# Order of the output products in two recurrent mixers

## The chip, the cores and the metric

The kernel runs on one core of a Trainium2 chip. The metric is the device time of one execution in microseconds. Of the kernel before there are three runs: 1267.03, 1274.09 and 1274.21 us, median 1274.09 us. Engines: PE is TensorE (PEld its weight loads), DVE VectorE, ACT ScalarE, POOL GpSimd, SP SyncE, which issues the DMAs.

## What is computed

One layer of a diffusion backbone in fp32, for 512 latent tokens of one request and 128 context tokens of another (640 in all, `NT`). A norm modulated by the conditioning, one input projection, four token mixers in parallel (pooling, Fourier, RWKV-7, GLA), a projection of each with a gated sum, an output projection, a second norm and an MLP. Cut to the two mixers that matter here:

```python
def step(S, inp):                                    # RWKV-7, a state of 64 x 64 for each of 4 heads
    sa = einsum('bhvk,bhk->bhv', S, -kk_t)
    S = S * w_t + sa[..., None] * (kk_t * a_t) + v_t[..., None] * k_t
    return S, einsum('bhvk,bhk->bhv', S, r_t)

def step(S, inp):                                    # GLA, a chunk at a time
    o = einsum('bhts,bhse->bhte', att, vc) + einsum('bhtd,bhde->bhte', qc * exp(bcum), S)
    S = exp(b_last)[..., None] * S + einsum('bhsd,bhse->bhde', kc * exp(b_last - bcum), vc)
    return S, o
```

Both run once forward and once backward over the tokens, and the two outputs are added. In both, an output is a sum of two products: one over the state that the chunk found (the "state product"), one over the tokens inside the chunk (the "token product").

## The kernel before

*The main stream.* All large matrix products are taken as three passes on a high and a low part of each operand. `load` fetches a block of weights by DMA (L241), `split` makes its two parts on ScalarE (L246) and VectorE (L247), and `terms` issues the passes (L368). The gates and the branch projections (`gate`, `branch`, `merged`) are such products too, and stand between the steps of the recurrent mixers in TensorE's instruction stream.

*The order.* Each engine works through its own list of instructions in order. A framework writes the lists when the kernel is built: it takes instructions by priority (the order of the program, with `hi()` ahead) and by its own estimate of when operands are ready. So the lists don't depend on the run, and an engine that reaches an instruction too early waits there with all that stands behind it.

*RWKV-7* (from L627) works on two heads at a time (`hp`), one in each half of the 128 partitions (`HR`, `par` 0 and 1), in chunks of 64 tokens. Everything that doesn't need the state is prepared for all chunks: `SL` and `AB` (products within a chunk, L772 to L778, from `big`, L756 to L758), the inverse `TT` and `BHT`. Then eight steps run over the chunks. The tile `x` holds for every chain and head the state over v's tokens and u's tokens over v's. A step does, on TensorE, `pp` (L910, state against `SL`), copied by VectorE (L913); `pu` (L924, against `TT`), copied by VectorE and ScalarE into `x` (L927, L928); and `pn` (L933, against `BHT`), added by VectorE to the decayed state (L939), which gives the `x` of the next step. GpSimd fills in the tokens of v (L847). Steps 0 and 1 work on four chains (forward and backward, of the latent and of the context tokens), steps 2 to 7 on two.

The outputs of a step are issued one step late (`late`), behind L933 and ahead of the next L910, those of the last two steps at the end. `outputs` writes one PSUM bank `po`: chain `i` has 64 columns, head `par` the partitions `HR[par]`. The state product (L898) has all 128 partitions as its rows and 64 columns, the token product (L899) the 64 partitions of its head and 64 columns. ScalarE copies the bank out (L901). With four chains these are 16 products, with two 8. After the last step the sum of both directions is normalised (L957 to L969).

*GLA* (from L974) prepares the products within tiles of 128 tokens (`att`, L1073 to L1080) and the states at the borders of the tiles (`st`, L1121 to L1126; L1129 for the final state), then sums the outputs (L1135 to L1148) for each half `j` of the channels into one PSUM bank for the four latent tiles and another for the context tile: two token products (L1142, one a head, 64 columns each) and, for the latent tiles, two state products over both directions (L1146). VectorE adds the bank to `og` (L1148); ScalarE squares it (L1159) for a norm whose sums are products again (L499).

Of the kernel before, what the change touches and what calls it, by code (L numbers as in the profile page):

```python
# [19 lines left out]
P = 128  # L20
D = 1024
KT = 8
NS = 512
# [4 lines left out]
EPS = 1e-6  # L28
# [32 lines left out]
def blocks(w, starts, n):  # L61
    """Blocks of n columns of w, each with a partition's rows next to one another."""
    return np.stack([w[:, c : c + n].reshape(-1, P, n).transpose(1, 0, 2) for c in starts])


def laid_out(x):
    """The weights and the small vectors in the order in which they are loaded."""
    return {
        "t_par": np.concatenate([np.reshape(x[n], (-1, P)) for n, _ in PARAMS]).T,
        "t_in": blocks(x["w_in"][0], W_TILES, P),  # L70
        "t_ada": blocks(x["ada_w"][0], range(0, 6 * D, 512), 512),
        "t_branch": np.stack([blocks(w, range(0, D, P), P) for w in x["w_branch"][0]]),
        "t_w1": blocks(x["mlp_w1"][0], range(0, FF, P), P),
        "t_w2": np.stack([blocks(x["mlp_w2"][0][r : r + 256], (0, 512), 512) for r in range(0, FF, 256)]),
        "t_out": blocks(x["w_out"][0], (0, 512), 512),
    }
# [60 lines left out]
def backbone(ctx, tc, a, y_prompt, y_sample, out_rwkv, out_gla):  # L137
# [6 lines left out]
    turn = [0]  # L144

    def first():
        """Ahead of all else, in the order of the calls."""
        turn[0] += 1
        return tc.high_priority(offset=1000000 - 1000 * turn[0])
# [7 lines left out]

# [1 line left out]
    cst = cpool.tile([P, NCST], F32, name="cst")  # L159
# [37 lines left out]

# [1 line left out]
    sc = cpool.tile([P, 2, KT], F32, name="sc")  # L199
# [29 lines left out]
    def blocks(src, pool=None, tag="w", bufs=2):  # L229
        """A block of weights, 128 rows to each k, as tiles for its two parts and a list of loads."""  # L230
        pool = wpool if pool is None else pool
        _, n, c = src.shape
        wh = pool.tile([P, n, c], F32R, name=tag + "h", tag=tag + "h", bufs=bufs)
        wl = pool.tile([P, n, c], F32R, name=tag + "l", tag=tag + "l", bufs=bufs)
        m = min(n, 512 // c)
        return wh, wl, [(src[:, k : k + m], wh[:, k : k + m], wl[:, k : k + m]) for k in range(0, n, m)]
# [7 lines left out]
    def split(raw, wh, wl):  # L244
        """Two parts that the tensor engine takes in one pass each."""
        S.copy(wh, raw)  # L246
        V.tensor_tensor(wl, raw, f32(wh), ALU.subtract)  # L247
# [15 lines left out]
    def ada_out(pc, part, hf, out):  # L263
        """(2, 512) sums, as columns [P, 4, 2], plus the bias and, for a scale, one, times the norm's gain."""
        kts = slice(hf * 4, hf * 4 + 4)

        def wide(t, o):
            return t[:, o + hf * 4 : o + hf * 4 + 4].unsqueeze(2).broadcast_to([P, 4, 2])

        if part in (1, 4):  # L270
            V.tensor_tensor(out[:, kts], pc, wide(bp1, part * 8), ALU.add)
            V.tensor_tensor(out[:, kts], out[:, kts], wide(pcol, PC["norm1_g" if part == 1 else "norm2_g"]), ALU.mult)
        else:
            V.tensor_tensor(out[:, kts], pc, wide(pcol, PC["ada_b"] + part * 8), ALU.add)

    def ada_mm(pool, pt, hf, part, k):
        """Two steps of half of the scale (1) or of the shift (0): rows of c and c_ctx, by the parts of sc."""
        raw = raws[part, hf, k]
# [12 lines left out]
    def ada_cols(pool, pt, hf):  # L291
        """The rows of the scale and the shift as per-partition columns."""
        with hi():
# [17 lines left out]
    def ada_sum(pt, acc, part, hf, out):  # L311
        """The sums over the partitions, as columns."""
        for k in range(4):
# [5 lines left out]
    def ada_rest(pool, bank, part, hf, bufs=2):  # L319
        """Half of another part, summed per partition on VectorE; returns what sums over the partitions."""  # L320
        c0 = part * D + hf * 512
# [19 lines left out]

# [1 line left out]
    def rstd_of(pool, ss, n):  # L343
        """1/sqrt(ss / D + EPS): a guess of its negative from the exponent's bits, and Newton steps that turn the sign."""
        h, y, z = (pool.tile([P, n], F32, name=f"rs{j}", tag=f"rs{j}", bufs=2) for j in range(3))
# [17 lines left out]
    def terms(pt, wh, wl, k, c0, mh, ml, start, stop):  # L363
        """pt += W.T @ m for one tile of 128 rows of W; wh/wl tiles [P, K, cols]."""
        lh, ll = wh[:, k, c0 : c0 + P], wl[:, k, c0 : c0 + P]
# [107 lines left out]

# [1 line left out]
    def proj(c0):  # L475
# [18 lines left out]
    def bank_pair(lhsT, rhs, bank=None):  # L494
        """Two banks of lhsT.T @ rhs over the two halves of the tokens."""
        r = []
# [9 lines left out]
    def rsqrt_of(lhs, eps, sqs, rss, bank=None):  # L506
        """rs = 1/sqrt(lhs.T @ sq + eps)."""
        for sq, rs in zip(sqs, rss):
# [5 lines left out]

# [1 line left out]
    apool = pf_.enter_context(tc.tile_pool(name="apool", bufs=1))  # L516
# [39 lines left out]

# [1 line left out]
    # Over the sample's tokens, the sums and the differences of t and NS - t: cosines of the ones, sines of the others.  # L558
    zc = [ft(512).rearrange("p (s j c) -> p s j c", s=2, j=2) for _ in range(3)]
# [38 lines left out]

# [1 line left out]
    uscr = [dpool.tile([P, NT], F32, name=f"uscr{n}") for n in range(len(UC))]  # L600
# [25 lines left out]

# [1 line left out]
    psa.close()  # L628
# [53 lines left out]
    def pick(t, step, smp):  # L682
        """The two directions' chunks of one step, of the samples or of the prompt."""
        return t[:, step : step + 13 : 12] if smp else t[:, 8 + step : 11 + step : 2]

    for hp in range(2):
# [65 lines left out]
        def pair(d, e, g0, g1):  # L752
            """(k, b, k) of a group of chunks, scaled by e."""
            n = g1 - g0
# [33 lines left out]

        # the 32x32 diagonal blocks of I - A, inverted with one block per partition
        ivf = upool.tile([80, 1024], F32, name="inv", tag="inv")  # L790
# [30 lines left out]

        # tokens of v per chunk
        vr = ut()
# [17 lines left out]
        def new_x(step):  # L841
            """Per chain and head: the state over v's tokens, and u's tokens over v's."""
            x = upool.tile([P, 4, 2, 2, 64], F32, name="xc", tag="xc", bufs=3)
# [45 lines left out]

        # the recurrence over the chunks  # L890
        O = [ut(), ut()]

        def outputs(x, live):
            po = pxc()
            for i, d, c in live:
                for par, R in enumerate(HR):
                    o64 = slice(i * 64, i * 64 + 64)
                    PE.matmul(po[R, o64], lhsT=x[:, i, par, 0, :], rhs=SL[d][:, par, c, 64:128], start=True, stop=False)  # L898
                    PE.matmul(po[R, o64], lhsT=x[R, i, par, 1, :], rhs=AB[d][R, c, 64:128], start=False, stop=True)  # L899
            for i, d, c in live:  # L900
# [72 lines left out]

# [1 line left out]
    pb.close()  # L975
# [159 lines left out]
    for j in range(2):  # L1135
        for t0, t1 in ((0, 4), (4, 5)):
            pt = pxt()
            for i in range(t0, t1):
                o = (i - t0) * P
                for r in range(2):  # L1140
                    h = 2 * j + r
                    PE.matmul(pt[64 * r : 64 * r + 64, o : o + P], lhsT=vtok[:, i, 64 * h : 64 * h + 64],  # L1142
                              rhs=att[:, h, i, :], start=True, stop=i == 4)
                if i < 4:
                    for d in range(2):
                        PE.matmul(pt[:, o : o + P], lhsT=st[d][i][:, j * P : j * P + P], rhs=qd[d][:, i * P : i * P + P],  # L1146
                                  start=False, stop=d == 1)
            V.tensor_tensor(og[j][:, t0 * P : t1 * P], og[j][:, t0 * P : t1 * P], pt[:, : (t1 - t0) * P], ALU.add)  # L1148
# [16 lines left out]

# [1 line left out]
    def load_y(n, pool=mgpool):  # L1167
# [97 lines left out]

# [1 line left out]
    late = ctx.enter_context(tc.tile_pool(name="late", bufs=1, side="right", reuse_waits="tile"))  # L1267
# [72 lines left out]

# [1 line left out]
    with tc.tile_pool(name="mlp", bufs=1, reuse_waits="tile") as mp, \  # L1342
# [57 lines left out]

        # the last half by tiles of tokens, each followed by its norm
        h2pool.close()
# [55 lines left out]
```

## Time and profile before

| | |
|---|---|
| runs | 1267.03, 1274.09, 1274.21 us |
| span of the profiled execution (the only time of it that the profile gives) | 1268.9 us |
| TensorE busy | 1226.0 us, 97% |
| VectorE busy | 733.4 us, 58% |
| ScalarE busy | 500.2 us, 39% |
| GpSimd busy | 60.6 us, 5% |
| TensorE's mean granted clock | 0.970 |
| RWKV-7 output products | 16 groups between 319.9 and 549.9 us |
| GLA output products | 671.5 to 686.3 us |

Times in the views are microseconds from the start of the span, means in ns. In a timeline a row is: start, length, engine, line, operation, output<-inputs, count, and in brackets the idle time before it with what ended it. A product in fp32 leaves two records in the trace, so x8 stands for four products, and products of a row overlap. PEclk is the share of its full clock that TensorE was granted. "issue" is idle time that no semaphore explains.

### The profile page before, as it was taken

What the parts mean: (1) busy time and instruction counts of PE and PEld (TensorE: products, weight loads), DVE (VectorE), ACT (ScalarE), POOL (GpSimd) and SP (SyncE); (2) the same over time, 40 slices, a digit from 0 to 9 for tenths busy, and PEclk for the clock granted to TensorE, in tenths of its full rate; (3) what the DMA queues carried; (4) which work ended last, traced back from release to release, by engine and by line L of the source; (5) the groups of instructions that cost most, each with busy time, mean ns of one, the idle gap of its engine ahead of it and who ended that gap; (6) DMA issues with size and microseconds to landing.
All of it is one profiled execution on the core that took longest, in us unless ns stands there. A gap on an engine that the chain in (4) does not pass through costs nothing.

```text
span 1268.9 us, 19637 instructions
## 1 busy us (share of the span) xinstructions
PE 1226.0 (97%) x7556; PEld 1053.3 (83%) x7556; DVE 733.4 (58%) x1458; ACT 500.2 (39%) x1024; POOL 60.6 (5%) x98
## 2 busy tenths in 40 slices
PE   7998999999999999999899999999999999999997
PEld 2778997898777798788568897899899889989985
DVE  4797768493478473236786866643354444335456
ACT  4722236633265522137734333643133123313432
POOL 0000002200004100020000000000000000000000
PEclk9999899999999699799999999999999999999999
DMA  9557652334213142034444653122222222222222
GB/s 354 194 169 255 220 177 74 92 98 115 66 33 119 57 142 80 28 100 166 129 158 132 214 183 127 67 84 67 83 79 72 67 85 83 71 78 84 68 92 83
DMA packets 85971, 147.41 MB, mean 116 GB/s; under 512 B 21693, under 2 KB 26206, under 8 KB 85878
## 3 DMA queue, kind: packets, MB, share of 16 engines
q1 hardware_dynamic: 85878, 146.16, 35.4%
q8 instruction: 59, 0.97, 0.3%
q14 instruction: 34, 0.28, 0.1%
HBM read 123.17 MB, written 22.95 MB: 115 GB/s over the span
## 4 chain that ended last, share of the span: by engine, by line
PE 44%; DVE 2%; DMA 2%; ACT 1%; issue 1%; SPq 0%; DVEq 0%; ACTq 0%
PE pf L1349 17%; PE pf L1395 15%; PE pt L368 3%; PE po L1235 3%; PE pf L1415 2%; PE px L1073 1%; DMA wr<-in_t_w_dram 1%; DMA wr<-in_t_in_dram 1%; DMA g1b<-grow 0%; PE px L1146 0%; DVE acc L309 0%; DMA araw<-in_t_ada_dram 0%; PE pf L1320 0%; DVE wl L247 0%; PE px L1142 0%
## 5 line engine op out<-in xcount | busy, mean ns | idle before, releaser
L247 DVE TENSOR_TENSOR wl<-wr,wh 128x512 fp32r<-128x512 f32 x222 | 151.1, 693 | 213.4 <-ACT wh L246 204.4
L246 ACT CAST wh<-wr 128x512 fp32r<-128x512 f32 x222 | 133.5, 618 | 352.1 <-PE pf L1395 139.3
L368 PE MATMUL pt<-xh,wh 128*128 128x320 f32 x816 | 202.5, 325 | 1.9 <-DVE grow L337 1.2
L368 PE MATMUL pt<-xl,wh 128*128 128x320 f32 x816 | 203.3, 325 | 0.0
L368 PE MATMUL pt<-xh,wl 128*128 128x320 f32 x816 | 200.4, 323 | 0.0
L1349 PE MATMUL pf<-nh,wl 128*128 128x320 f32 x512 | 158.1, 309 | 0.0
L1349 PE MATMUL pf<-nl,wh 128*128 128x320 f32 x512 | 158.0, 309 | 0.0
L1349 PE MATMUL pf<-nh,wh 128*128 128x320 f32 x512 | 157.9, 309 | 0.0
L368 PEld LDWEIGHTS pt<-xh,wh 128*128 128x128 f32 x816 | 141.0, 194 | 10.8 <-issue 3.5
L368 PEld LDWEIGHTS pt<-xl,wh 128*128 128x128 f32 x816 | 141.5, 194 | 7.6 <-issue 3.9
L368 PEld LDWEIGHTS pt<-xh,wl 128*128 128x128 f32 x816 | 142.0, 195 | 5.0 <-issue 2.0
L1395 PE MATMUL pf<-wl,fh 128*128 128x512 f32 x280 | 109.0, 389 | 0.0
L1395 PE MATMUL pf<-wh,fh 128*128 128x512 f32 x280 | 109.0, 389 | 0.0
L1395 PE MATMUL pf<-wh,fl 128*128 128x512 f32 x280 | 108.9, 389 | 0.0
L1349 PEld LDWEIGHTS pf<-nl,wh 128*128 128x128 f32 x512 | 96.0, 188 | 0.2
L1349 PEld LDWEIGHTS pf<-nh,wh 128*128 128x128 f32 x512 | 96.0, 188 | 0.1
L1349 PEld LDWEIGHTS pf<-nh,wl 128*128 128x128 f32 x512 | 96.0, 188 | 0.0
L309 DVE SCALAR_TENSOR_TENSOR acc<-araw,sc,acc 128x512 f32<-128x512 f32 x112 | 78.4, 744 | 11.9 <-DMA araw<-in_t_ada_dram 11.9
L1395 PEld LDWEIGHTS pf<-wh,fl 128*128 128x128 f32 x280 | 52.6, 188 | 11.0
L1395 PEld LDWEIGHTS pf<-wh,fh 128*128 128x128 f32 x280 | 52.6, 188 | 10.9
L1395 PEld LDWEIGHTS pf<-wl,fh 128*128 128x128 f32 x280 | 52.6, 188 | 10.7
L1354 DVE TENSOR_TENSOR rl<-rl,pf 128x320 f32<-128x320 f32 x64 | 30.9, 483 | 39.0 <-ACT rl L1353 39.0
(538 smaller groups left out, 1826.5 us busy)
## 6 DMA issues: line engine op xcount, KB each, us to landing
wr<-in_t_w_dram SPq DMA_DIRECT2D x128, 256.0 KB, 3.1
wr<-in_t_in_dram SPq DMA_DIRECT2D x102, 256.0 KB, 3.2
araw<-in_t_ada_dram SPq DMA_DIRECT2D x64, 256.0 KB, 3.4
adaw<-in_t_ada_dram SPq DMA_DIRECT2D x16, 512.0 KB, 9.2
mscr<-gate SPq DMA_DIRECT2D x24, 320.0 KB, 4.1
mg<-mscr SPq DMA_DIRECT2D x24, 320.0 KB, 3.4
uscr<-mg SPq DMA_DIRECT2D x15, 320.0 KB, 2.2
wr<-in_t_branch_dram SPq DMA_DIRECT2D x32, 128.0 KB, 2.2
```

The source lines that it names most:

```text
L246: S.copy(wh, raw)
L247: V.tensor_tensor(wl, raw, f32(wh), ALU.subtract)
L309: V.scalar_tensor_tensor(acc[j], raw, w, acc[j], ALU.mult, ALU.add)
L368: PE.matmul(pt[:, b, :HN], lhsT=w, rhs=m[:, b * HN : b * HN + HN], start=start and n == 0, stop=stop and n == 2)
L1073: PE.matmul(pt, lhsT=ek[:, ts_], rhs=em[:, :, ts_], start=True, stop=True)
L1235: PE.matmul(acc, lhsT=m[k][:, sl_], rhs=W[k, hf][w][:, 0, :], start=k == 0 and n == 0, stop=k == KT - 1 and n == 2)
L1349: PE.matmul(pt[:, :HN], lhsT=wk[:, k, :], rhs=m[:, k, bs], start=k == 0 and n == 0, stop=k == KT - 1 and n == 2)
L1354: V.tensor_tensor(rl, rl, pt[:, :HN], ALU.mult)
L1395: PE.matmul(acc[i], lhsT=m[k][:, ts_], rhs=w[:, kk, :], start=k == 0 and n == 0, stop=k == 7 and n == 2)
L1415: PE.matmul(acc, lhsT=m[k][:, ts_], rhs=ws[k][w][:, 0, :], start=k == 0 and n == 0, stop=k == 7 and n == 2)
```

## The change

In `outputs` the two products of a chain and head no longer follow one another. First come the state products of all chains and heads, then all token products. A product that opens a sum marks the PSUM bank (in its half of the partitions) as empty, so only the first state product of each head opens (`start=n == 0`), and only the last chain's token products close. All else writes where nothing was written or adds where something was. In the GLA sums the order is the other way round: the token products of all tiles of a bank first, of which the first of each head opens, then the state products. The number of products, their operands and the copies stay as they were. The removed comments and docstrings change nothing, but the changed functions are longer: behind L895 line numbers of the kernel after are larger by 4, from the GLA sums on by 5 (L910 becomes L914, L1146 L1151); the token products of `outputs` become L902.

```diff
         def outputs(x, live):
             po = pxc()
-            for i, d, c in live:
+
+            for n, (i, d, c) in enumerate(live):
                 for par, R in enumerate(HR):
-                    o64 = slice(i * 64, i * 64 + 64)
-                    PE.matmul(po[R, o64], lhsT=x[:, i, par, 0, :], rhs=SL[d][:, par, c, 64:128], start=True, stop=False)
-                    PE.matmul(po[R, o64], lhsT=x[R, i, par, 1, :], rhs=AB[d][R, c, 64:128], start=False, stop=True)
+                    PE.matmul(po[R, i * 64 : i * 64 + 64], lhsT=x[:, i, par, 0, :], rhs=SL[d][:, par, c, 64:128],
+                              start=n == 0, stop=False, skip_group_check=True)
+            for n, (i, d, c) in enumerate(live):
+                for par, R in enumerate(HR):
+                    PE.matmul(po[R, i * 64 : i * 64 + 64], lhsT=x[R, i, par, 1, :], rhs=AB[d][R, c, 64:128],
+                              start=False, stop=n == len(live) - 1, skip_group_check=True)
             for i, d, c in live:
                 S.copy(rv(O[d], d)[:, c * 64 : c * 64 + 64], po[:, i * 64 : i * 64 + 64])
...
                 for r in range(2):
                     h = 2 * j + r
                     PE.matmul(pt[64 * r : 64 * r + 64, o : o + P], lhsT=vtok[:, i, 64 * h : 64 * h + 64],
-                              rhs=att[:, h, i, :], start=True, stop=i == 4)
-                if i < 4:
-                    for d in range(2):
-                        PE.matmul(pt[:, o : o + P], lhsT=st[d][i][:, j * P : j * P + P], rhs=qd[d][:, i * P : i * P + P],
-                                  start=False, stop=d == 1)
+                              rhs=att[:, h, i, :], start=i == t0, stop=i == 4, skip_group_check=True)
+            for i in range(t0, min(t1, 4)):
+                o = (i - t0) * P
+                for d in range(2):
+                    PE.matmul(pt[:, o : o + P], lhsT=st[d][i][:, j * P : j * P + P], rhs=qd[d][:, i * P : i * P + P],
+                              start=False, stop=d == 1 and i == 3, skip_group_check=True)
```

How this stands in TensorE's list, before, at the end of the first four-chain group of the first head pair (`sl_1562` and `sl_1605` are the `SL` of the two directions, `ab_1614` and `ab_1681` their `AB`; `pxc` are PSUM banks):

```order
L898 MATMUL pxc_2173<-sl_1562,xc_1954 64x64
L899 MATMUL pxc_2173<-ab_1614,xc_1954 64x64
L898 MATMUL pxc_2173<-sl_1605,xc_1954 64x64
L899 MATMUL pxc_2173<-ab_1681,xc_1954 64x64
L898 MATMUL pxc_2173<-sl_1605,xc_1954 64x64
L899 MATMUL pxc_2173<-ab_1681,xc_1954 64x64
L910 MATMUL pxc_2194<-xc_2159,sl_1562 64x64 x2
L910 MATMUL pxc_2194<-xc_2159,sl_1605 64x64 x2
L368 MATMUL pt_5068<-xh5_125,wh_5058 128x320 x2
```

And the same place, the whole group, after:

```order
L898 MATMUL pxc_2173<-sl_1562,xc_1954 64x64 x2
L898 MATMUL pxc_2173<-sl_1605,xc_1954 64x64 x2
L898 MATMUL pxc_2173<-sl_1562,xc_1954 64x64 x2
L898 MATMUL pxc_2173<-sl_1605,xc_1954 64x64 x2
L902 MATMUL pxc_2173<-ab_1614,xc_1954 64x64 x2
L902 MATMUL pxc_2173<-ab_1681,xc_1954 64x64 x2
L902 MATMUL pxc_2173<-ab_1614,xc_1954 64x64 x2
L902 MATMUL pxc_2173<-ab_1681,xc_1954 64x64 x2
L914 MATMUL pxc_2194<-xc_2159,sl_1562 64x64 x2
L914 MATMUL pxc_2194<-xc_2159,sl_1605 64x64 x2
L368 MATMUL pt_5068<-xh5_125,wh_5058 128x320 x2
```

The 16 products became two runs of eight; what stands ahead of and behind them is the same, and so it is at the other 15 groups and on every other engine up to the GLA sums.

There more has moved. TensorE's list before, in the middle of the GLA sums (`px_4470` is the bank of the latent tiles of `j` = 0, `px_4492` that of `j` = 1; `gs` are the states, `gt` the scaled queries):

```order
L368 MATMUL pt_6721<-xh2_122,wl_6712 128x320 x2
L1146 MATMUL px_4470<-gt_4419,gs_4460 128x128
L1142 MATMUL px_4470<-att_4068,vtok_4111 64x128 x2
L1146 MATMUL px_4470<-gt_4368,gs_4397 128x128
L1146 MATMUL px_4470<-gt_4419,gs_4454 128x128
L1142 MATMUL px_4470<-att_4068,vtok_4111 64x128 x2
L1146 MATMUL px_4470<-gt_4368,gs_4403 128x128
```

And after, where the sums begin (numbers of tiles left out):

```order
L1146 MATMUL px<-att,vtok 64x128 x8
L1151 MATMUL px<-gt,gs 128x128
L1146 MATMUL px<-att,vtok 64x128 x2
L368 MATMUL pt<-xl_135,wh 128x320 x2
L368 MATMUL pt<-xh_127,wl 128x320 x2
L1146 MATMUL px<-att,vtok 64x128 x8
L1151 MATMUL px<-gt,gs 128x128
L1146 MATMUL px<-att,vtok 64x128 x2
L368 MATMUL pt<-xh_120,wh 128x320 x2
```

All token products now stand at the beginning, with one state product behind each of the two runs of eight; 17 products of the main stream follow, and then the other 14 state products in one run. Behind the GLA sums some gates, loads of weights and parts of the last modulation (L309, L325, L335) change places by a few rows on TensorE, ScalarE, VectorE and SP.

## The prediction

> **What bounds the kernel now.** I read the page first, then the tensor engine's waits, then its timeline through both recurrences and the end of the GLA mixer, then busy time by stretches.
>
> ```profile
> span 1268.9 us, 19637 instructions
> PE 1226.0 (97%) x7556; PEld 1053.3 (83%) x7556; DVE 733.4 (58%) x1458; ACT 500.2 (39%) x1024; POOL 60.6 (5%) x98
> ```
>
> TensorE is busy 97% of the span and no other engine passes 58%. Busy is not the same as used, though, so the next view is one stretch for each situation that matters here (the RWKV output products in 319.9 to 324, the preparation of the second head pair in 372 to 405, and stretches at half clock):
>
> ```profile
> core 0: us, PE busy (x) PEld busy (x) DVE busy (x) ACT busy (x) POOL busy (x), PEclk, DMA share, GB/s
> 319.90:324.00 4.10, 4.10 (x33) 3.03 (x32) 0.08 (x1) 0.36 (x1) 0.00 (x0) 1.00 0.22 49
> 331.90:335.40 3.50, 3.50 (x20) 2.60 (x18) 1.79 (x6) 1.74 (x3) 0.36 (x1) 0.51 0.02 5
> 372.00:405.00 33.00, 30.16 (x191) 26.36 (x189) 32.55 (x52) 22.86 (x43) 11.78 (x12) 1.00 0.36 106
> 506.00:523.00 17.00, 17.00 (x97) 12.71 (x97) 3.68 (x10) 3.37 (x13) 1.58 (x4) 0.50 0.15 51
> 523.00:550.00 27.00, 27.00 (x240) 20.07 (x240) 7.60 (x24) 4.47 (x18) 2.90 (x8) 1.00 0.10 33
> ```
>
> In the recurrences TensorE is busy without a gap while VectorE works 7.6 of 27 us (second head pair): there its instruction stream alone sets the pace. In 372 to 405 VectorE is the full one (32.55 of 33 us). The lines that the change touches are L898 and L899:
>
> ```profile
> L898 PE MATMUL pxc<-sl,xc x160: 222/222/367, 319.9 to 549.4; 128*64 128x64 f32 x160
> L899 PE MATMUL pxc<-ab,xc x160: 218/267/366, 320.2 to 549.7; 64*64 64x64 f32 x160
> ```
>
> Each product leaves two records, so these are 80 state and 80 token products. What one costs is read from start to start, since ends are modelled:
>
> ```profile
> 320.18 0.33 PE L899 MATMUL pxc<-ab,xc 64*64 64x64 f32 x2
> 320.44 0.33 PE L898 MATMUL pxc<-sl,xc 128*64 128x64 f32 x2
> ...
> 323.77 0.33 PE L899 MATMUL pxc<-ab,xc 64*64 64x64 f32 x2
> 324.03 0.45 PE L910 MATMUL pxc<-xc,sl 128*64 128x64 f32 x8
> 324.41 0.56 PE L368 MATMUL pt<-xh,wh 128*128 128x320 f32 x2
> ...
> 325.19 0.45 PE L924 MATMUL pxc<-p,TT 64*64 64x64 f32 x8
> 325.57 0.57 PE L368 MATMUL pt<-xh,wl 128*128 128x320 f32 x2
> ```
>
> While state and token products alternate, a product takes 0.257 us (15 of them from 320.18 to 324.03). Four products of one kind in a row take 0.38 us in all, with the change of kind behind them: L910 has the shape of the state products (128 rows on 64 columns), L924 that of the token products (64 on 64). That is 0.095 us each. A longer run:
>
> ```profile
> 499.93 0.68 PE L933 MATMUL pxc<-xc,bht 128*64 128x64 f32 x14
> 500.54 0.56 PE L368 MATMUL pt<-xl,wh 128*128 128x320 f32 x2
> ```
>
> Seven products (14 records) take 0.61 us, so a further record costs (0.61 - 0.38) / 6 = 0.038 us, and a run of eight products 0.38 + 8 x 0.038 = 0.69 us.
>
> **The change part by part.** *RWKV outputs.* There are 16 groups: in each of two head pairs two with four chunks (16 products) and six with two (8 products). Now: 160 x 0.257 = 41.1 us. After: four groups of two runs of eight, 8 x 0.69 = 5.5 us, and twelve groups of two runs of four, 24 x 0.38 = 9.1 us; together 14.6 us. Saved: 26.5 us, all of it on TensorE. Below, the token products could lose their overlap (a rival).
>
> One group ran at half clock:
>
> ```profile
> 513.36 0.47 PE L899 MATMUL pxc<-ab,xc 64*64 64x64 f32 x2
> 513.76 0.47 PE L898 MATMUL pxc<-sl,xc 128*64 128x64 f32 x2
> ...
> 518.60 0.69 PE L910 MATMUL pxc<-xc,sl 128*64 128x64 f32 x8
> 519.23 0.64 PE L368 MATMUL pt<-xl,wh 128*128 128x320 f32 x1
> ```
>
> 13 products in 5.24 us are 0.403 us each, so its 16 cost 16 x (0.403 - 0.257) = 2.3 us more than I have counted; shortened and at full clock they don't: saved 2.3 us. If the half-clock stretches themselves go, the other work in them gets faster by 0.38 / 0.63 (the two L910 rows): 17 - 6.4 (that group, 16 x 0.403) = 10.6 us would become 6.4, and the 3.5 us from 331.9 become 2.1, 5.6 us in all. Both stretches begin about as a four-chunk group ends, but the group of 319.9 was followed by none, so I leave this out of the sum and put 5.6 us into the low end.
>
> *What was hidden behind the outputs.* They stand between the state update (L933) and the next step's first product (L910), which needs VectorE's sum L939:
>
> ```profile
> 534.56 0.39 PE L933 MATMUL pxc<-xc,bht 128*64 128x64 f32 x5
> 535.21 0.60 DVE L939 TENSOR_TENSOR xc<-xf,pxc 64x128 f32<-64x128 f32 x2 [1.64 <-PE pxc L933]
> ...
> 536.74 0.56 PE L368 MATMUL pt<-xh,wl 128*128 128x320 f32 x2
> 537.23 0.45 PE L910 MATMUL pxc<-xc,sl 128*64 128x64 f32 x8
> ```
>
> The last three L933 products and four state products are one run of seven, 0.61 us; the token run 0.38; the two L368 products 0.49 (536.74 to 537.23). L910 could then start at 534.56 + 1.48 = 536.04, and L939 ends at 535.81: 0.23 us of cover remain where there were 1.4. Where L910 follows a four-chunk group directly: eleven products of one kind, 0.38 + 14 x 0.038 = 0.91, and 0.69 make 1.60 us, against 1.25 for L939. So no wait on paper; I add 0.5 us for the whole, and up to 1 us in each of the twelve groups before an L910 as a rival. ScalarE's copies (L901) and GpSimd's refill of x (L847) start when the token run ends, so earlier by what is saved. No DMA is added; in the RWKV part every queue keeps its order, around the GLA end a few loads on SP change places.
>
> *The next stage.* After the first head pair VectorE is full, and TensorE waits for it there:
>
> ```profile
> PE px L772 <- DVE big L757: 2.0, 1, 2.0
> PE px L772 <- ACT big L758: 1.1, 1, 1.1
> 369.19 1.29 DVE L247 TENSOR_TENSOR wl<-wr,wh 128x512 fp32r<-128x512 f32 x2 [2.52 <-issue]
> ```
>
> VectorE's full stretch starts behind the last outputs with these splits of weights, whose buffers TensorE frees, so it starts earlier by the same 13 us; these 3.1 us stay and nothing is lost to them.
>
> *GLA outputs.* 20 token and 16 state products:
>
> ```profile
> L1142 PE MATMUL px<-att,vtok x40: 272/298/323, 671.5 to 685.3; 128*64 128x128 f32 x40
> L1146 PE MATMUL px<-gt,gs x32: 272/275/377, 671.9 to 685.9; 128*128 128x128 f32 x32
> 678.58 0.71 PE L1146 MATMUL px<-gt,gs 128*128 128x128 f32 x4
> 679.22 0.44 PE L1142 MATMUL px<-att,vtok 128*64 128x128 f32 x4
> 679.59 0.71 PE L1146 MATMUL px<-gt,gs 128*128 128x128 f32 x4
> ...
> 680.60 0.94 PE L1146 MATMUL px<-gt,gs 128*128 128x128 f32 x6
> 681.46 0.44 PE L1142 MATMUL px<-att,vtok 128*64 128x128 f32 x4
> ```
>
> State products: 0.64 us for four records, 0.86 for six, so 0.11 a record and 0.20 a run; nine runs become three, 6 x 0.20 = 1.2 us saved. Token pairs: 0.37 us each, ten of them; eight fall into two runs of 16 records, at about 0.05 a further record (half of 0.11, two column halves side by side, an estimate) 0.37 + 12 x 0.05 = 1.0 us a run where four pairs take 1.5: another 1.0 us. Together 2.2 us, between 0 and 3: the state products now stand in one run of 14, and if a state on VectorE is late, all of that run waits for it.
>
> **The sum.** 1268.9 - 26.5 - 2.3 - 2.2 + 0.5 = 1238.4 us for the profiled execution. The three runs were 1267.0, 1274.1 and 1274.2, so that execution lies 5.2 us below the median and near the fastest. I can't tell which kind the median after will be and add half, 2.6: **1241 us**.
>
> **The rivals.** *The cover is gone* (0.10): in the first head pair VectorE has preparation of the second between the steps, L939 stands behind it, and TensorE waits at L910 up to 1 us in each of twelve steps. For it: only 0.23 us are left. Against it: L939 started at once after L933 in the rows above. 1241 + 12 = 1253.
>
> *The token products don't overlap* (0.06): two row halves of the array write one PSUM bank, and the second waits for the first; the 80 token products keep 0.257 us, 20.6 instead of 7.3, so 13.3 us of the gain go: 1254. Against it: L924 does just this, into one tile of one bank, and its run takes the 0.38 us of L910, which uses all rows. The Trainium skill (TensorEngine Tiling (Array Packing), Restrictions and Gotchas) says that different row tiles cannot access the same PSUM bank simultaneously. By that rule it would come out at this rival's time; the L924 row speaks against it.
>
> *It doesn't do what it says* (0.05): the 0.257 us belong to these products, not to the change of kind, say because they accumulate where L910 and L924 each open and close. No row shows a run of accumulating products of these two shapes. Then nothing changes: about 1272, with GLA's 2.2.
>
> *Slower: the clock* (0.04): where TensorE now waits within steps, its clock is granted at half through both recurrences. They last 50 + 48 us (319 to 369, 502 to 550), 70 without what the change takes out; at 0.63 / 0.38 that is 46 us more: 1241 + 46 = 1287. It decides from about 50 us at half clock on, where the 33 us of gain are eaten. For it: 17 us at 0.50 followed the group of 502. Against it: that followed a dense stretch without waits, and the change makes such stretches shorter. The Trainium skill (TensorE: Matmul & The Clock Gate, Part 1) says that an idle window of about 3.4 us brings the half rate. By that rule the waits would have to be far longer than the 1 us above; the trace's own half-clock stretches began without such a gap.
>
> **How the numbers follow.** The forecast, 1230 to 1252, has 0.75. Low end: the fastest run, 1267.0, less 31 and less 5.6 gives 1230. High end: both 1253 and 1254 and half of the 5.2 around them, 1256. What is left out is the last two rivals and the tails, some 0.18. A measurement of this kernel tells 1% from no change, 12.7 us: under 1261 counts as faster. Forecast and the first two rivals are faster, less 0.02 for two of them at once: 0.89; same 0.07; slower 0.04.
>
> **What would show it.** Right: the state and token lines in runs, next product kind 0.38 us after a run of four and about 0.69 after one of eight; all groups together near 15 us; L910 without waits; TensorE's span shorter by 13 us at the end of either recurrence, with the clock at 1.00 from 506 on the old scale or not. Wrong: token runs of four over 0.8 us (no overlap), waits of L910 for L939, or new waits in the preparation stage or at the GLA end that give back what the recurrences gained.

## The result, and the profile after

| | before | after |
|---|---|---|
| median of the runs | 1274.15 us (1267.03 to 1277.8, 4 runs) | 1236.78 us (1222.49 to 1242.74, 4 runs) |
| ratio to before, 95% interval (without the run of 1242.74) | | 0.967 [0.959, 0.975] |
| the profiled execution's span | 1268.9 us | 1241.0 us |

The kernel is 3% faster. The profiled execution of the kernel after is the longest of its four runs, 1242.74 us, at a lower mean clock (0.971) than the other three (0.978 to 0.990), and is left out of the ratio. Its page:

```profile
span 1241.0 us, 19640 instructions
PE 1194.1 (96%) x7556; PEld 1032.8 (83%) x7556; DVE 734.0 (59%) x1458; ACT 500.5 (40%) x1024; POOL 61.8 (5%) x98
```

TensorE still bounds the kernel; VectorE's and ScalarE's work is what it was. The timeline of TensorE shows a group with four chains (from 494.95) and one with two, whose state products begin among the last L937 (the old L933) and whose token products stand at 504.54:

```profile
494.95 0.69 PE L898 MATMUL pxc<-sl,xc 128*64 128x64 f32 x16
495.57 0.68 PE L902 MATMUL pxc<-ab,xc 64*64 64x64 f32 x16
496.18 0.45 PE L914 MATMUL pxc<-xc,sl 128*64 128x64 f32 x8
...
504.54 0.45 PE L902 MATMUL pxc<-ab,xc 64*64 64x64 f32 x8
504.92 0.42 PE L368 MATMUL pt<-xh,wh 128*128 128x320 f32 x1
```

A run of eight takes 0.61 to 0.62 us, a run of four 0.38, and the next step's first product (L914) starts at once behind them. All 16 groups together, each from its first record to the start of what follows, took 42.97 us before and take 14.58 us after.

Busy time by stretches, first before, then after: from the first output product of the first head pair to the end of its outputs, from there to the first of the second pair (its preparation), and from there to the end.

```profile
319.92:368.68 48.76, 48.76 (x391) 35.51 (x390) 24.05 (x59) 19.00 (x46) 5.69 (x13) 0.97 0.14 43
368.68:502.02 133.34, 129.97 (x964) 112.73 (x962) 87.62 (x187) 60.91 (x135) 21.51 (x30) 0.90 0.34 102
502.02:549.85 47.83, 47.83 (x366) 35.59 (x365) 11.34 (x35) 8.15 (x31) 4.33 (x12) 0.82 0.12 38
```

```profile
327.48:362.50 35.02, 34.56 (x391) 25.85 (x390) 23.73 (x59) 18.64 (x46) 6.60 (x13) 1.00 0.20 60
362.50:494.95 132.45, 128.75 (x965) 111.58 (x962) 88.21 (x188) 61.27 (x136) 21.52 (x30) 0.91 0.36 103
494.95:523.15 28.20, 28.20 (x365) 22.05 (x365) 11.96 (x35) 8.15 (x31) 4.53 (x12) 1.00 0.21 65
```

The two recurrences became shorter by 13.74 and 19.63 us, 33.4 in all, with the same work in them, and TensorE's clock in them (the number behind the five engines) is 1.00 where it was 0.97 and 0.82. A second profile of the kernel after, from a run of 1230.02 us (`e7_after_again`), gives the same two lengths:

```profile
317.13:352.15 35.02, 34.56 (x390) 25.84 (x389) 23.75 (x59) 18.64 (x46) 6.62 (x13) 1.00 0.19 60
484.61:512.83 28.22, 28.22 (x366) 22.07 (x365) 11.96 (x35) 8.16 (x31) 4.54 (x12) 1.00 0.20 65
```

In the first TensorE now has 0.46 us without work; nearly all of it is one wait for VectorE:

```profile
334.86 0.45 PE L928 MATMUL pxc<-p,TT 64*64 64x64 f32 x8 [0.40 <-DVE ut L674]
```

The preparation between them is where it was, up to 0.9 us. The whole difference of the two profiled executions is 27.9 us: the recurrences gave 33.4, the preparation 0.9, the stretch from the last RWKV output to the first GLA sum 3.0 (121.65 to 118.65; 6.8 us of it ran at half clock before, none after); what stands ahead of the first output group took 7.6 more (319.92 to 327.48), and what follows from the first GLA sum to the last product 1.8 more. The order ahead of the outputs is unchanged, but TensorE's clock wasn't the same there, first before, then after:

```profile
0.00:319.92 319.92, 303.51 (x1996) 256.33 (x1996) 220.15 (x443) 136.49 (x263) 22.02 (x39) 0.97 0.52 174
```

```profile
0.00:327.48 327.48, 309.89 (x1996) 261.38 (x1997) 219.87 (x443) 136.62 (x263) 22.26 (x39) 0.95 0.52 170
```

It was at half for 17.1 us before and for 34.1 after, and that is most of the 7.6 (the price of half clock is worked out further below). It isn't the change: in the other profiles below, with the same order ahead, the first group starts between 317.0 and 323.6.

From the first GLA sum to the last product, before and then after:

```profile
671.50:1259.20 587.70, 583.93 (x3300) 526.61 (x3300) 304.13 (x585) 202.93 (x413) 0.00 (x0) 1.00 0.29 96
```

```profile
641.80:1231.30 589.50, 582.97 (x3300) 528.08 (x3300) 304.19 (x585) 203.00 (x413) 0.00 (x0) 0.99 0.30 95
```

The GLA products did become cheaper. TensorE's timeline after, at both ends of them:

```profile
641.76 1.09 PE L1146 MATMUL px<-att,vtok 128*64 128x128 f32 x16
642.78 0.49 PE L1151 MATMUL px<-gt,gs 128*128 128x128 f32 x2
...
648.76 3.29 PE L1151 MATMUL px<-gt,gs 128*128 128x128 f32 x28
651.81 0.39 PE L368 MATMUL pt<-xh,wl 128*128 128x320 f32 x1
```

A token run of 16 records takes 1.02 us, the state run of 28 records 3.05. From each record's start to the next, the 72 records sum to 6.67 us, against 9.45 before: 2.8 us less. But a wait stands behind them, in TensorE's waits of the whole span before (first fence) and after (total, times, longest). Before, all five stand ahead of the sums; the sixth is new:

```profile
PE pt L368 <- ACT bh L246: 4.3, 5, 2.8
```

```profile
PE pt L368 <- ACT bh L246: 8.5, 6, 4.1
```

The timelines of ScalarE and TensorE after show the new one. `bh` is the high part of a branch's weights, `wo70h` and `wo71h` those of the output projection:

```profile
724.49 0.62 ACT L246 CAST wo70h<-wr 128x512 fp32r<-128x512 f32 x1 [3.51 <-DMA wr<-in_t_out_dram]
...
729.95 0.62 ACT L246 CAST wo71h<-wr 128x512 fp32r<-128x512 f32 x1 [4.23 <-DMA wr<-in_t_out_dram]
730.47 0.40 ACT L246 CAST bh<-wr 128x256 fp32r<-128x256 f32 x1
```

```profile
730.93 0.90 PE L368 MATMUL pt<-yh,bh 128*128 128x320 f32 x2 [4.07 <-ACT bh L246]
```

In ScalarE's new list both `wo70h` and `wo71h` come ahead of the last two `bh`; before, one `bh` stood between them. `wo71h` waits 4.23 us for its load, `bh` stands behind it, and TensorE behind `bh`. A stretch at half clock begins in this wait too:

```profile
729.20:736.00 6.80, 5.02 (x16) 4.33 (x17) 3.63 (x6) 2.11 (x5) 0.00 (x0) 0.50 0.88 325
```

### The profile page after: what moved, and what is told of

Read it like the earlier page. It is cut to its first block, busy times and chain, and to the rows that moved or that the text cites. A ratio compares the mean times of both kernels' runs of the same rounds, so it can differ in the third digit from the quotient of the medians.

```text
span 1241.0 us, 19640 instructions
## 1 busy us (share of the span) xinstructions
PE 1194.1 (96%) x7556; PEld 1032.8 (83%) x7556; DVE 734.0 (59%) x1458; ACT 500.5 (40%) x1024; POOL 61.8 (5%) x98
## 4 chain that ended last, share of the span: by engine, by line
PE 43%; DMA 3%; DVE 3%; ACT 2%; issue 1%; DVEq 0%; ACTq 0%
PE pf L1354 18%; PE pf L1400 15%; PE po L1240 4%; PE pf L1420 2%; DMA wr<-in_t_out_dram 2%; PE px L1077 2%; DMA wr<-in_t_in_dram 1%; PE pt L368 1%; DVE acc L309 1%; DVE wl L247 0%; ACT eqm L1073 0%; PE pf L1325 0%; PE px L1151 0%; DVE gate L1202 0%; DMA mg<-mscr 0%
## 5 line engine op out<-in xcount | busy, mean ns | idle before, releaser
L368 PEld LDWEIGHTS pt<-xh,wh 128*128 128x128 f32 x816 | 140.1, 192 | 8.8 <-issue 4.0
L309 DVE SCALAR_TENSOR_TENSOR acc<-araw,sc,acc 128x512 f32<-128x512 f32 x112 | 78.4, 744 | 12.5 <-DMA araw<-in_t_ada_dram 12.4
```

The source lines that it names most:

```text
L309: V.scalar_tensor_tensor(acc[j], raw, w, acc[j], ALU.mult, ALU.add)
L368: PE.matmul(pt[:, b, :HN], lhsT=w, rhs=m[:, b * HN : b * HN + HN], start=start and n == 0, stop=stop and n == 2)
```

## The experiments

Two questions: which part of the change carries the gain, and what makes an alternating product so dear. My theory at this point was that the RWKV part carries it, and that a product costs 0.257 us because the next one has another shape. The rival to the second half was that a token product waits for the sum that its state product has just left in the same columns. All short diffs are against the kernel after.

### The RWKV part alone, and the GLA part alone

The first has the GLA sums of the kernel before, the second its `outputs`:

```diff
-                              rhs=att[:, h, i, :], start=i == t0, stop=i == 4, skip_group_check=True)
-            for i in range(t0, min(t1, 4)):
-                o = (i - t0) * P
-                for d in range(2):
...
+                              rhs=att[:, h, i, :], start=True, stop=i == 4)
+                if i < 4:
+                    for d in range(2):
...
```

> RWKV part alone, GLA sums as before. Theory (a change of the product's shape costs TensorE a fixed time, and the RWKV groups hold nearly all of them): the 16 groups take 14.6 us as in the changed kernel, the span shrinks by about 28 us against before, and the 4.1 us wait of TensorE near 731 us in the changed kernel (a branch's weights behind late loads of the output weights) is absent, since the lists behind the GLA sums are those of before: 1228 to 1240 us, equal to the changed kernel or up to 7 us faster. Rival (the GLA part carries a share of the gain): slower than the changed kernel by 2 us or more, 1239 to 1250 us.

> GLA part alone, RWKV outputs as before. Theory: the 16 groups take about 43 us again; the GLA sums get 1 to 3 us shorter on TensorE, and the wait of about 4 us for a branch's weights behind them appears in this kernel too, since it comes from the reordered lists: 1270 to 1282 us, no change that can be measured. Rival (the wait came from TensorE arriving earlier): no such wait, 1266 to 1274 us.

The RWKV part alone took 1230.91 us (1223.66 to 1235.56, 6 runs), ratio 0.9675 [0.9624, 0.9725]; its groups sum to 14.58 us. The GLA part alone took 1276.03 us (1265.43 to 1283.41, 10 runs), ratio 1.0027 [0.9988, 1.0065]: no change. It has a wait of 4.06 us for `bh` at 768.6 too, so that wait comes with the GLA part and not with the shorter recurrences. Its own recurrences, untouched, are the ones of before:

```profile
317.67:369.90 52.23, 52.23 (x391) 37.45 (x390) 24.17 (x59) 18.98 (x46) 5.70 (x13) 0.88 0.13 40
505.80:559.00 53.20, 53.20 (x365) 39.23 (x364) 11.20 (x35) 8.25 (x31) 4.29 (x12) 0.71 0.11 34
```

They took 8.84 us longer than in the profile of before, at lower clocks (0.88 and 0.71): 42.8 us of them ran at half clock, against 20.5.

### Pairs, and state and token product apart

Two orders between before and after. In the first, each chain's two state products (both heads) are followed by its two token products:

```diff
-            for n, (i, d, c) in enumerate(live):
+            for i, d, c in live:
...
-                              start=n == 0, stop=False, skip_group_check=True)
-            for n, (i, d, c) in enumerate(live):
+                              start=True, stop=False, skip_group_check=True)
...
```

In the second, state and token products alternate as before, but a token product comes three products behind its state product (one, with two chains), so that it never adds to what has just been written:

```diff
...
+            for m in range(len(todo) + lag):
+                if m < len(todo):
+                    state(*todo[m])
+                if m >= lag:
+                    token(*todo[m - lag])
...
```

`state` and `token` are functions that issue the one and the other product, `todo` lists the chains and heads in their old order, `lag` is 3 or 1.

> RWKV outputs by chain: the state products of both heads, then the token products of both heads, each state product opening its own sum as before; half the changes of shape of before. GLA as in the changed kernel. Theory (a fixed time for each change of shape, two products of a kind side by side): a run of two products 0.38 - 4 x 0.038 = 0.23 us, so 0.46 us a chain: groups of four chains 1.84 us, of two 0.92 us, about 18.4 us in all. Rival (a token product waits for the state product it adds to, whatever the shape): the token products still stand right behind theirs, a chain takes about 0.5 to 0.8 us, 20 to 32 us in all.

> RWKV outputs with state and token products still alternating, but each token product behind a state product of another chain (three products later in groups of four chains, one later in groups of two). GLA as in the changed kernel. Theory (the change of shape costs): 0.257 us for each product that stands alone between two of the other kind, a run of four 0.38 and of two 0.23: groups of four chains 8 x 0.257 + 2 x 0.38 = 2.82 us, of two chains 4 x 0.257 + 2 x 0.23 = 1.49 us, 29 us in all. Rival (a token product waits for the sum it adds to): with that sum long written nothing is waited for, 1.3 us and 0.8 us, about 15 us in all.

Pairs took 1252.66 us, apart 1250.52 (one run each). TensorE's timeline of a group with four chains, pairs first:

```profile
498.41 0.34 PE L897 MATMUL pxc<-sl,xc 128*64 128x64 f32 x4
498.68 0.33 PE L900 MATMUL pxc<-ab,xc 64*64 64x64 f32 x4
...
500.25 0.33 PE L900 MATMUL pxc<-ab,xc 64*64 64x64 f32 x4
500.52 0.45 PE L912 MATMUL pxc<-xc,sl 128*64 128x64 f32 x8
```

```profile
493.51 0.45 PE L900 MATMUL pxc<-sl,xc 128*64 128x64 f32 x8
493.90 0.33 PE L905 MATMUL pxc<-ab,xc 64*64 64x64 f32 x2
494.15 0.33 PE L900 MATMUL pxc<-sl,xc 128*64 128x64 f32 x2
...
496.33 0.45 PE L923 MATMUL pxc<-xc,sl 128*64 128x64 f32 x8
```

Two products side by side take 0.264 us (2.11 us for eight runs), hardly more than one alone (0.25 to 0.26 in the second fence). With four chains the second order takes 2.82 us where the theory said 2.82 and the rival 1.3: distance from the open sum doesn't help. With two chains it takes 1.61 us where the theory said 1.49. The pairs cost more than I expected (22.8 us for all groups, two of them at half clock, not 18.4), since I had read a run of two off a straight line through runs of four and seven, 0.23 us. All of it follows from three prices, read between starts of records: a change of kind costs 0.150 us, a product 0.107 if it is alone in its run and 0.058 if the two heads' products run side by side. Four chains give 16 x (0.107 + 0.150) = 4.1 before, 8 x 0.150 + 16 x 0.058 = 2.13 for pairs (measured 2.11), and 2 x 0.150 + 16 x 0.058 = 1.23 after (1.23).

### One shape, and one head after the other

These separate the change of shape from the two heads side by side. In the first, state and token products alternate exactly as before, but the token product takes 128 rows like the state product. What the kernel then computes for RWKV isn't the layer's output; it serves for the times alone:

```diff
...
-                    PE.matmul(po[R, i * 64 : i * 64 + 64], lhsT=x[R, i, par, 1, :], rhs=AB[d][R, c, 64:128],
-                              start=False, stop=n == len(live) - 1, skip_group_check=True)
+                    PE.matmul(po[R, i * 64 : i * 64 + 64], lhsT=x[:, i, par, 1, :], rhs=AB[d][:, c, 64:128],
+                              start=False, stop=True)
```

In the second, both runs go through all chains of head 0 and then of head 1:

```diff
-            for n, (i, d, c) in enumerate(live):
-                for par, R in enumerate(HR):
+            for par, R in enumerate(HR):
+                for n, (i, d, c) in enumerate(live):
...
```

> State and token products alternate as in the kernel before, but the token product takes all 128 partitions as its rows, like the state product (its other 64 rows then multiply the other head's columns, so what this kernel computes for RWKV isn't the reference's). GLA as in the kernel after. Theory (the change of shape costs, 0.15 us at each): there is none here, a product costs what it costs in a run, 0.058 us where the two heads lie side by side and at most 0.107 where both of its records follow one another in the same columns: a group with four chains 1.0 to 1.8 us, one with two 0.6 to 1.0. Rival (the token product waits for the sum that the state product has just left in the same columns): 0.257 us for each product as before, 4.1 and 2.05 us.

> By kind as in the kernel after, but each run goes through all chains of head 0 and then through all of head 1, so that consecutive products write the same half of the partitions and can't lie side by side. The number of changes of kind is that of the kernel after. GLA as in the kernel after. If the two heads' products lying side by side gives part of the gain: a record follows another 0.053 us later where it shares the columns of the array (the second record of a product follows its first so), a run of eight takes 16 x 0.053 = 0.85 and the step to the next kind 0.10: about 1.9 us for a group with four chains, 1.0 for one with two. Rival (the change of shape is all): 1.23 and 0.76 as in the kernel after. Rival (side by side is all): 4.1 and 2.05 as in the kernel before.

One shape took 1234.56 us, by head 1230.58 (one run each; the argument rests on the rows, not on these times). Their groups with four chains, one shape first:

```profile
485.51 0.34 PE L897 MATMUL pxc<-sl,xc 128*64 128x64 f32 x4
485.68 0.29 PE L899 MATMUL pxc<-ab,xc 128*64 128x64 f32 x4
485.80 0.33 PE L897 MATMUL pxc<-sl,xc 128*64 128x64 f32 x4
...
486.50 0.45 PE L911 MATMUL pxc<-xc,sl 128*64 128x64 f32 x8
```

```profile
479.64 0.97 PE L897 MATMUL pxc<-sl,xc 128*64 128x64 f32 x16
480.53 0.96 PE L901 MATMUL pxc<-ab,xc 64*64 64x64 f32 x16
481.43 0.45 PE L913 MATMUL pxc<-xc,sl 128*64 128x64 f32 x8
```

With one shape the old order costs 0.99 us a group instead of 4.1, less than the new order (1.23), although every token product still adds to the columns that its state product has written just ahead of it; a state and a token product together take 0.12 us, twice the 0.058 of a product in a run. So the rival is dead, and the change of shape is shown to be the cost. The Trainium skill (TensorEngine Tiling (Array Packing), Tiling Modes, Key Properties) says that switching the tiling mode, not just the tile, drains the TensorE; these rows agree, and put 0.150 us on it for 64-column fp32 products.

By head, a run of eight takes 0.89 us instead of 0.61, so the two heads side by side are worth the other 0.28. I had expected 0.95. The starts of its 16 records show why it is less: three of them still fall beside records of the other head, at the border between the two, so that they take 13 places of 58 ns (0.75 us, and 0.150 for the change). With two chains (runs of four) by head costs no more than the kernel after, 0.82 and 0.77 us a group against 0.81 and 0.76; I had expected 1.0.

### The kernel after and the RWKV part alone on one chip

> The kernel after once more, on the same chip as the next run. Theory (the gain is RWKV's alone; what GLA gains is given back behind it): 1232 to 1242 us, 0 to 6 us slower than the next run, with the 4 us wait for the branch weights behind the GLA sums. Rival (GLA gives 2 us too, and what stood between the two before was chance of the clock): 2 us faster than the next run.

> The kernel after with the GLA sums of the kernel before (the RWKV part alone), once more beside the kernel after. Theory: 1228 to 1236 us, 0 to 6 us faster than the kernel after, no wait of 4 us behind the GLA sums. Rival: 2 us slower than the kernel after.

The kernel after took 1233.14 us (1230.02 to 1235.68, 6 runs), ratio 0.9686 [0.9647, 0.9725]; the RWKV part alone 1234.87 us (1232.34 to 1237.47, 6 runs), 0.9695 [0.9658, 0.9731]. The times can't tell them apart, so neither beats the other. Nor do their profiles over the stretch in which they differ: from the first GLA sum to the last product 588.2 us in the kernel after (a wait of 3.4 us for `bh`) and 588.1 with the old GLA sums:

```profile
630.40:1218.60 588.20, 582.28 (x3300) 527.43 (x3300) 304.30 (x585) 203.02 (x413) 0.00 (x0) 1.00 0.30 95
```

```profile
636.20:1224.30 588.10, 584.34 (x3300) 526.38 (x3300) 304.57 (x585) 202.94 (x413) 0.00 (x0) 1.00 0.30 96
```

Over all profiles so far this stretch lasts 587.1, 587.7 and 588.1 us in the three with the old sums, and 588.2 to 589.8 in the seven with the new ones. The 2.8 us that the sums gained are not there; the new sums are 0 to 2.7 us slower in it. All seven have the wait for `bh`, 3.4 to 4.1 us, and a stretch of 3.4 to 6.8 us at half clock that begins in it or up to 1.8 us behind it; the three have neither. At 0.41 us for each us at half clock (worked out below) that clock costs another 1.4 to 2.8 us. A wait of 0.8 to 1.0 us for VectorE's `ot` further on, which the three have, is gone in the seven.

### The wait for `bh` taken away

```diff
-            for hf in range(2):
-                W[dt, hf] = load(a["t_out"][hf, :, dt : dt + 1], mxpool, f"wo{dt}{hf}", 1)
+        if 0 < dt <= KT:
+            for hf in range(2):
+                W[dt - 1, hf] = load(a["t_out"][hf, :, dt - 1 : dt], mxpool, f"wo{dt - 1}{hf}", 1)
```

> The kernel after, with the loads of the output projection's weights asked for one step of the loop later, so that the last branch weights (bh) stand ahead of the last output weights (wo70, wo71) on SyncE and ScalarE, as in the kernel before. The computation is the same. Theory (the wait of 3.4 to 4.1 us for bh behind the GLA sums, which comes from the order of the lists, is what gives GLA's gain back): the wait goes, with the stretch at half clock that begins at it; from the first GLA sum to the last product 584 to 586 us instead of 588.2 to 589.5, 1228 to 1233 us in all. Rival (the loads themselves are late, whatever their order): a wait of the same length turns up at another load, and the stretch stays at 588 to 590 us.

It took 1236.87 us (1234.23 to 1244.12, 6 runs), ratio 0.9736 [0.9693, 0.9779]: in time no better than the kernel after. Its profile, for the same stretch, and TensorE's waits of 1 us and more in it for other than `bh`:

```profile
640.10:1226.50 586.40, 581.55 (x3300) 526.03 (x3300) 304.25 (x585) 203.01 (x413) 0.00 (x0) 1.00 0.30 96
```

```profile
745.00 0.50 PE L1240 MATMUL po<-wo01h,mh 128*128 128x512 f32 x1 [2.51 <-DVE ot L1301]
```

The waits for `bh` in the whole span are back at 4.3 us, as before, no stretch at half clock begins there, and the stretch takes 586.4 us, 1.8 to 3.3 less than with the new list. That is between the theory (584 to 586) and the rival (588 to 590), because a part has moved: TensorE waits 2.51 us at 745.00 for VectorE's `ot`, where it was 1.0 before. So the order of the loads does cause the wait for `bh`, but with it gone only part of the 2.8 us that the sums gained is there: 586.4 is 0.7 to 1.7 us under the profiles with the old sums. This is one profile. At that place TensorE doesn't set the pace alone.

## Why the prediction was right

**The groups.** Predicted from 41.1 to 14.6 us at full clock; measured 14.58. With the one group at half clock, 26.5 + 2.3 = 28.8 us were to be saved; 42.97 - 14.58 = 28.4 were. Runs of eight were put at 0.69 and took 0.61 to 0.62; on the other side eight of the twelve groups with two chains, those that begin among L937's records, took 0.81 instead of 0.76. The errors cancel. That the step from a run of four to one of eight could be read off L910, L924 and L933 held, since these are the same two shapes. Reading a run of two off the same line did not (0.264, not 0.23); the prediction didn't use one.

**The total.** The forecast was 1241 us, and the medians came out at 1236.8 and 1233.1. That the profiled execution spans just 1241.0 is chance: its clock ahead of the first outputs cost it 7 us more than before, nearly as much as the clock gained in the recurrences (8.4, below). One slip in the working changes nothing: its upper end adds up to 1256 us, and the range is stated to 1252.

**The clock.** Here is the term that was mis-sized: of the 5.6 us that the rest of the half-clock stretches would give, the prediction says "I leave this out of the sum and put 5.6 us into the low end". They did go: no profile of a kernel with products by kind, or with one shape, has half clock in the recurrences; seven of seven. What half clock costs can be read from the preparation of the second pair, which is the same work in all kernels; by head it ran at full clock, in the pairs kernel at 0.85:

```profile
356.80:479.60 122.80, 119.11 (x964) 104.41 (x962) 88.89 (x188) 61.12 (x136) 21.67 (x30) 1.00 0.38 111
```

```profile
358.30:498.40 140.10, 136.60 (x964) 118.10 (x962) 87.48 (x187) 61.04 (x135) 21.64 (x30) 0.85 0.33 97
```

A clock of 0.85 over 140.1 us is half clock for 0.30 of it, 42 us, and costs 17.3: 0.41 us each. Over all eleven profiles this stretch takes 122.8 us and 0.40 more for each us at half clock. Before, the recurrences had 3.4 + 17.1 = 20.5 us of it, worth 8.4. So of the 33.4 us gained there, 25.0 are work at full clock (the prediction's 26.5 - 0.5 = 26.0) and 8.4 are the clock (its 2.3, and the 5.6 that it left out, 7.9). With the 5.6 in the sum, 1241 becomes 1235, between the two medians measured, 1236.8 and 1233.1.

**The cover.** It held: L914 follows L902 without a wait, with 0.23 us in hand on paper. The one new wait is 0.40 us at L928 for preparation on VectorE, near the 0.5 us allowed.

**The next stage.** Neutral, as predicted: 133.34 us at a clock of 0.90, 132.45 at 0.91.

**GLA.** Predicted 2.2 us, 0 to 3. In place the products gave 2.8 (state runs 1.5, token runs 1.3). But the term for the whole has the other sign: 0 to 2.7 us slower from the sums to the last product. The step that failed is "around the GLA end a few loads on SP change places", costed at nothing: the framework wrote other lists behind the shorter sums, a load for the branch came behind two larger ones, and TensorE waits 3.4 to 4.1 us for it where it hadn't waited, with 3.4 to 6.8 us at half clock from there. The prediction had named such a wait only as a sign of being wrong.

**The rivals.** The token products do overlap across two row halves of one bank: their run of eight takes 0.61 us, the state products' 0.62, and the records of the two row halves start 7 ns apart (495.569 and 495.576 us). Each half writes its own partitions of the bank. The Trainium skill's rule (TensorEngine Tiling (Array Packing), Restrictions and Gotchas), by which such tiles can't access one bank at once, doesn't cost anything that these rows show. That the 0.257 us belong to accumulating products fell with the same rows: the token products accumulate there too. The slower clock went the other way: in the recurrences it rose. The lost cover would have shown as waits of L914 for L943, the old L939; there is none in either recurrence.

## What to carry to other kernels

Small products of two shapes that alternate pay a change of shape each, here 0.150 us beside 0.058 us of work; sort them by shape, or give them one shape, and put the two column halves next to one another. Before the price of a short run is taken from a longer one, look for a run of that length in the trace. Where a framework writes the instruction lists, an edit that saves 3 us in one place rewrites the order of loads behind it, and what that costs has to be read from the new lists, load by load; it can be as much as the gain.

## What I had not expected of the hardware

A product alone between two of another shape costs as much as two side by side (0.257 and 0.264 us), and alternating products of one shape that add to the same columns cost nothing extra (0.99 us for 16, against 16 x 0.058 = 0.93).

Stretches at half clock began in the recurrences of four kernels, or directly behind them, and these are the four that change shape most often (before, GLA part alone, pairs, apart): at 331.9 and 506.0; 357.7, 518.2 and 559.1; 349.8; and 355.1 us. Each of the seven begins between 0.2 us ahead of and 0.8 us behind the end of an output group, and in the 7 us before each TensorE had been busy without a gap. In the seven other profiles none begins there. The Trainium skill (TensorE: Matmul & The Clock Gate, Part 1) ties the half rate to an idle window of about 3.4 us. The seven last 3.4 to 30.7 us, multiples of 3.4, which agrees, and so do the waits of 3.4 to 4.1 us for `bh` with half clock behind them; but no idle time stands ahead of the seven.

That so many changes of shape count as idle would fit; it was not isolated, and only the coincidence is shown. The traces hold a hint at what counts. All half-clock stretches of one profile begin on one grid of 3.413 us (506.02 - 331.94 us is 51 times that). Cut the recurrences into windows by that grid, and count in each the columns that TensorE's records streamed, times the share of the 128 rows that they used. The seven windows that end where the clock fell have 1280 to 2112, and so have only three others at full clock; in the seven profiles without such a stretch no window has under 2336. That is a count chosen after the fact, so it doesn't show a rule. Changes of shape aren't the only such place either: without a gap in the 7 us before, half clock also began in the preparation of two kernels (pairs at 482.9, apart at 478.0 us) and ahead of the recurrences of the kernel after (at 251.3 us).

The same half clock, 0 to 42 us of it in the preparation and 7 to 34 us ahead of the first outputs, is also most of what makes runs of one kernel differ (the kernel before on one chip: 1265.36 us at a mean clock of 0.975, 1280.72 at 0.960): a time of this kernel is compared with its clock beside it, or over several runs.
